# Output projection: the next tile's load and split are written ahead of the present tile's matmuls

## The chip, the cores and the metric

The kernel runs on one core of a Trainium2 chip. A core has a matmul engine (TensorE, PE in the profile; its weight loads are PEld), a vector engine (VectorE, DVE), an activation engine (ScalarE, ACT), GpSimd (POOL) and a queue for issuing DMAs (SyncE, SP). The metric is the device time of one launch in microseconds.

## The reference

One layer of a streaming encoder over 2048 prompt frames, 16 meta tokens and 32 sample frames. Cut to the lines that matter:

```python
q, k, v, z_a, b_g, c_g, u, z_c = split_proj(rmsnorm(hp, norm_g[l]), w_in[l])
...
o = rmsnorm(o, sub_g) * (1.0 - lam_init)
o = o.reshape(*o.shape[:2], W_ATT) * jax.nn.silu(z_a)
y_c = jax.nn.silu(z_c) * b_g * conv_out
return jnp.concatenate([o, y_c], axis=-1) @ w_o
...
y_prompt = rmsnorm(hp[:, N_META:], final_g)
y_sample = rmsnorm(hd, final_g)
```

`o` comes from differential attention with four heads, `conv_out` from a short gated convolution. The concatenation is 1024 wide, `w_o` is 1024x1024; its product is added to the residual `hp`, and the sum goes through a last RMSNorm. The change touches only this last product and what surrounds it.

## The kernel before, in words

Inputs and weights are f32. Each matmul is done in three terms on operands that are split into a high and a low part (hi x hi, lo x hi, hi x lo): the hi part is a cast on ScalarE, the lo part a subtraction on VectorE or GpSimd.

The kernel first runs the input projection and the attention for four blocks of 512 frames and four heads, and leaves the concatenation, transposed, in DRAM (`cat`, one piece for each block; `cat_s` for the sample frames). At the end stands the output projection over tiles of 128 frames: 16 prompt tiles (0 to 13, then 15 and 16 by their place in the list below) and one tile of 32 sample rows (place 14). In this document a tile is named by its place in that list. The columns of the result are done in two halves of 512:

- `out_first` (L700) does the first half of tiles 0 to 11 and puts the sums in DRAM (`y0`), together with the sums of squares of each row. It is spread through the attention work of the last block.
- `out_rest` (L709) does the second half of tiles 0 to 11, then both halves of places 12 to 16, normalises and stores.

For each tile `load_cat` (L660) loads 512 KB of `cat` into a `wraw` buffer, of which there are two, and splits it in two pairs. In `out_rest` the even places put the pairs in `chh` and `cll` (tags `wh`, `wl`, four buffers each) with the lo part on GpSimd. The odd places, called spare, put both in `cs` tiles of the tag `p0`, with the lo part on VectorE. The tag `p0` has twelve buffers (`NP[0]`), and the two result tiles `y` of each tile are `p0` tiles too. A new `p0` tile takes the slot of the oldest, and its writer waits until the last user of that one is done; for a `y` that is its store.

`half_product` (L678) runs 24 matmuls of 128x512 into PSUM, adds the sum to `y` on VectorE (L694) and squares and accumulates it on ScalarE (L695). In `out_rest` L727 adds the sums of squares, `rsqrt` (L178 to L184) goes VectorE, ScalarE twice (L179, L180), VectorE four times (L181 to L184), and L731 scales each half before its store.

All DMAs are issued by SP, in order (L80). The order of the instructions on each engine is fixed when the kernel is built: a scheduler places every instruction from its dependences, and the order in which the code is written is its priority. Each engine then runs its row in order and waits at the head for what is missing.

Of the kernel before, what the change touches and what calls it, by code (L numbers as in the profile page):

```python
# [47 lines left out]
def hybrid_step(ctx: ExitStack, tc: tile.TileContext, x, xT, ckT, cv, scT, rel_bias, norm_g, w_in,  # L48
# [24 lines left out]
    def halved(out, a, b, op, engine=None):  # L73

        n = out.shape[-1] if len(out.shape) == 2 else out.shape[1]
        cuts = (0, n // 2, n) if engine is None and n * (out.shape[-1] if len(out.shape) > 2 else 1) > 256 else (0, n)
        for c0, c1 in zip(cuts, cuts[1:]):
            (engine or G).tensor_tensor(out[:, c0:c1], a[:, c0:c1], b[:, c0:c1], op=op)  # L78
# [97 lines left out]
    def rsqrt(r, ssum, var, w, scale):  # L176

        V.tensor_scalar(var, ssum, scale, EPS, op0=ALU.mult, op1=ALU.add)  # L178
        S.activation(r, var, AF.Ln)  # L179
        S.activation(r, r, AF.Exp, scale=-0.5)  # L180
        V.tensor_tensor(w, r, r, op=ALU.mult)  # L181
        V.tensor_tensor(w, w, var, op=ALU.mult)
        V.tensor_scalar(w, w, -0.5, 1.5, op0=ALU.mult, op1=ALU.add)
        V.tensor_tensor(r, r, w, op=ALU.mult)  # L184
# [459 lines left out]
    def w_half(n):  # L644
        if n == 0:
            his = [xp.tile([P, NX + QT], F32R, tag=f"xh{k}", name=f"woh{k}")[:, :512] for k in range(KT)]
            los = [xp.tile([P, NX + QT], F32R, tag=f"xl{k}", name=f"wol{k}")[:, :512] for k in range(KT)]
        else:
            ks = [ks_tile(c) for c in range(2)]
            his = [ks[k // 4][:, 512 * (k % 4):512 * (k % 4 + 1)] for k in range(KT)]  # L650
            los = [one.tile([P, QT], F32R, tag=f"q{c}{i}", name=f"wq{c}{i}", bufs=2) for _ in range(2) for c in range(2)
                   for i in range(2)]
        for k in range(KT):
            wr = g_tile(512) if n == 1 and k >= 4 else one.tile([P, QT], F32, tag="xt", name="wr", bufs=XB)
            dma(wr, w_out[P * k:P * (k + 1), 512 * n:512 * (n + 1)])
            S.copy(his[k], wr)
            (G if k % 2 else V).tensor_tensor(los[k], wr, f32(his[k]), op=ALU.subtract)
        return his, los

    def load_cat(t, rows, spare=False):  # L660
        ct = wp.tile([P, KT, P], F32, tag="wraw", name="ct")
        dma(ct[:, :, :rows], cat_s if t == 16 else cat[t // 4][:, t % 4])
        parts = []
        for i in range(2):
            c = ct[:, 4 * i:4 * i + 4, :rows]
            if spare:
                chh, cll = [pp.tile([P, 4, P], F32R, tag="p0", name="cs", bufs=NP[0]) for _ in range(2)]
            else:
                chh = wp.tile([P, 4, P], F32R, tag="wh", name="chh", bufs=4)
                cll = wp.tile([P, 4, P], F32R, tag="wl", name="cll", bufs=4) if t < 16 else chh  # L670
            S.copy(chh[:, :, :rows], c)  # L671
            lo = cll[:, :, :rows] if t < 16 else cll[:, :, rows:2 * rows]
            halved(lo, c, f32(chh[:, :, :rows]), ALU.subtract, V if spare or t == 16 else None)
            parts.append((chh, cll))
        hi, lo = ([parts[k // 4][j][:, k % 4] for k in range(KT)] for j in range(2))
        return hi, lo if t < 16 else None

    def half_product(y, c, w, rows, ssq, more=False):  # L678

        chh, cll = c  # L680
        ps = (ps_s if more else ps_j).tile([P, 512], F32, tag="s" if more else "pj", name="po")
        if cll is None:
            for k in range(KT):
                for i in range(2):
                    T.matmul(ps[:2 * rows], lhsT=chh[k][:, :2 * rows], rhs=w[i][k],  # L685
                             start=(k == 0 and i == 0), stop=(k == KT - 1 and i == 1))
            lo = g_tile(512)[:rows]
            S.copy(lo, ps[rows:2 * rows])
            V.tensor_tensor(y, lo, y, op=ALU.add)
        ps = ps[:rows]  # L690
        for k in range(KT if cll is not None else 0):
            for i, (a, b) in enumerate(((chh, w[0]), (cll, w[0]), (chh, w[1]))):
                T.matmul(ps, lhsT=a[k][:, :rows], rhs=b[k], start=(k == 0 and i == 0), stop=(k == KT - 1 and i == 2))  # L693
        V.tensor_tensor(y, ps, y, op=ALU.add)  # L694
        S.activation(g_tile(512)[:rows], y, AF.Square, accum_out=ssq)  # L695

    def rows_of(t):
        return (NS, 0) if t == 16 else (P, NX + P * t)

    def out_first(ts, w):  # L700
        for t in ts:
            rows, x0 = rows_of(t)
            c = load_cat(t, rows)
            y = g_tile(512)[:rows]
            dma(y, x[x0:x0 + rows, :512])
            half_product(y, c, w, rows, ssq0[:rows, t:t + 1])
            dma(y0[t][:rows], y)

    def out_rest(ts, done, w0):  # L709
        w1 = w_half(1)  # L710
        fg = [pp.tile([P, 512], F32, tag="p1", name="fg", bufs=NP[1]) for _ in range(2)]
        for n in range(2):
            dma(fg[n], final_g[512 * n:512 * (n + 1)].partition_broadcast(P))
        for t in ts:
            rows, x0 = rows_of(t)
            c = load_cat(t, rows, ts.index(t) % 2 == 1)
            y = [pp.tile([P, 512], F32, tag="p0", name="y", bufs=NP[0])[:rows] for _ in range(2)]
            if t in done:
                dma(y[0], y0[t][:rows])
            else:  # L720
                dma(y[0], x[x0:x0 + rows, :512])
                half_product(y[0], c, w0, rows, ssq0[:rows, t:t + 1])
            dma(y[1], x[x0:x0 + rows, 512:])
            ss = sm.tile([P, 1], F32, tag="ss", name="ss")[:rows]
            half_product(y[1], c, w1, rows, ss, True)
            var, rs, w = (sm.tile([P, 1], F32, tag=f"y{i}", name=f"y{i}")[:rows] for i in range(3))
            V.tensor_tensor(ss, ss, ssq0[:rows, t:t + 1], op=ALU.add)  # L727
            rsqrt(rs, ss, var, w, 1.0 / D)
            dst = y_s if t == 16 else y_p[P * t:P * (t + 1)]
            for n in range(2):  # L730
                V.scalar_tensor_tensor(y[n], y[n], rs, fg[n][:rows], op0=ALU.mult, op1=ALU.mult)  # L731
                dma(dst[:, 512 * n:512 * (n + 1)], y[n])
# [27 lines left out]
    w0 = w_half(0)  # L760
    first = list(range(12))
    out_first(first, w0)
    out_rest(list(range(12)) + [12, 13, 16, 14, 15], first, w0)

_INS = ["x", "xT", "ckT", "cv", "scT", "rel_bias", "norm_g", "w_in", "conv_w", "lam_in", "subln_g", "w_out",
# [47 lines left out]
```

## Time and profile before

| | |
|---|---|
| time, three runs | 1292.02, 1292.07, 1293.26 us, median 1292.07 |
| profiled execution | 1293.26 us, its span 1291.5 us |
| TensorE busy | 1267.5 us (98%), mean granted clock 0.995 |
| VectorE, ScalarE, GpSimd busy | 923.9 us (72%), 827.5 us (64%), 699.0 us (54%) |
| DMA | 198.74 MB, 154 GB/s |
| chain that ended last | TensorE 55%, VectorE 3%, DMA 3%, ScalarE 1% |

The busy shares are means over the whole span. The span is from the first to the last instruction; the profiled execution's own time is 1.8 us longer. The output projection's second half takes the last 150 us.

### The profile page before, as it was taken

The page shows a single profiled execution, that of the slowest core. Times are in us where ns is not written, and L with a number is a line of the kernel's source. Part 1 is how long each engine was busy: PE and PEld are TensorE (multiplying, and loading weights), DVE is VectorE, ACT ScalarE, POOL GpSimd, SP SyncE. Part 2 cuts the span into 40 slices and gives each one's busy share as a digit, 9 for nine tenths or more (in the row PEclk, how much of TensorE's full clock was granted, in tenths as well). Part 3 has the DMA queues.
Part 4 walks back from the last instruction along what each step waited for, and adds up shares of the span by engine and source line. Part 5 has one row for each costly group of instructions (what it writes and reads, how often), then busy time and mean ns, then how long its engine had stood idle before and what let it go on. Part 6 is the DMA issues. An engine that isn't in the chain of part 4 may idle for free.

```text
span 1291.5 us, 21630 instructions
## 1 busy us (share of the span) xinstructions
PE 1267.5 (98%) x7058; PEld 1101.4 (85%) x7058; DVE 923.9 (72%) x2086; ACT 827.5 (64%) x2030; POOL 699.0 (54%) x918
## 2 busy tenths in 40 slices
PE   8999999999999998999999999999999999999897
PEld 6999999988888886888888888888888888888675
DVE  8767566567886847787878677767786896856654
ACT  6745454675776647677767567777777786763322
POOL 5775857767565675455556555364656483432200
PEclk9999999999999999999999999999999999999999
DMA  9834444774445347444343453344334543557652
GB/s 290 226 116 129 141 112 116 216 241 149 137 117 159 125 145 228 156 137 134 101 169 124 142 177 114 116 147 119 117 109 141 177 133 124 177 181 237 215 181 81
DMA packets 108048, 198.74 MB, mean 154 GB/s; under 512 B 17408, under 2 KB 45600, under 8 KB 107936
## 3 DMA queue, kind: packets, MB, share of 16 engines
q1 hardware_dynamic: 107936, 197.37, 49.0%
q8 instruction: 55, 0.90, 0.3%
q14 instruction: 57, 0.47, 0.1%
HBM read 145.62 MB, written 43.26 MB: 146 GB/s over the span
## 4 chain that ended last, share of the span: by engine, by line
PE 55%; DVE 3%; DMA 3%; ACT 1%; issue 1%; DVEq 0%; SPq 0%; ACTq 0%
PE pj L225 27%; PE po L693 9%; PE s L446 4%; PE s L447 4%; PE pt L462 3%; PE po L469 2%; PE po L471 2%; PE po L470 2%; DMA out<-y 1%; DMA ct<-cat 1%; PE po L685 1%; DMA y<-y 0%; DVE y L731 0%; PE ptv L316 0%; DVE cs L78 0%
## 5 line engine op out<-in xcount | busy, mean ns | idle before, releaser
L78 POOL TENSOR_TENSOR wl<-wr,wh 128x256 fp32r<-128x256 f32 x480 | 377.4, 810 | 300.6 <-ACT wh L204 279.4
L225 PE MATMUL pj<-xh,wh 128*128 128x512 f32 (+2 forms) x1280 | 456.9, 358 | 3.0 <-DVE g L352 1.3
L225 PE MATMUL pj<-xl,wh 128*128 128x512 f32 (+2 forms) x1280 | 453.6, 355 | 0.9 <-DVE xl L153 0.9
L225 PE MATMUL pj<-xh,wl 128*128 128x512 f32 (+2 forms) x1280 | 452.9, 354 | 0.0
L225 PEld LDWEIGHTS pj<-xh,wh 128*128 128x128 f32 x1280 | 242.5, 190 | 34.8 <-issue 2.3
L225 PEld LDWEIGHTS pj<-xh,wl 128*128 128x128 f32 x1280 | 242.2, 189 | 29.9 <-issue 0.2
L225 PEld LDWEIGHTS pj<-xl,wh 128*128 128x128 f32 x1280 | 242.4, 189 | 29.5 <-DVE xl L153 1.4
L397 ACT ACTIVATE p<-s,nm 128x384 f32<-128x384 f32 (+5 forms) x352 | 208.6, 595 | 68.8 <-DVE nm L396 41.9
L204 ACT CAST wh<-wr 128x512 fp32r<-128x512 f32 x256 | 157.5, 618 | 102.7 <-PE pj L225 72.0
L401 DVE SCALAR_TENSOR_TENSOR p<-p,cf,p 128x384 f32<-128x384 f32 (+5 forms) x176 | 127.1, 751 | 23.9 <-ACT p L400 23.7
L396 DVE TENSOR_REDUCE nm<-s 128x1 f32<-128x384 f32 (+3 forms) x224 | 122.6, 560 | 22.7 <-PE s L447 22.5
L78 POOL TENSOR_TENSOR cll<-ct,chh 128x256 fp32r<-128x256 f32 x80 | 63.1, 815 | 131.2 <-ACT chh L671 131.2
L466 DVE TENSOR_TENSOR al<-pt,ah 128x512 fp32r<-128x512 f32 x144 | 97.2, 684 | 46.7 <-ACT ah L465 46.1
L446 PE MATMUL s<-ks,q 128*128 128x384 f32 (+5 forms) x352 | 127.3, 363 | 1.0 <-ACT p L397 0.8
L447 PE MATMUL s<-ks,q 128*128 128x384 f32 (+5 forms) x352 | 122.5, 349 | 0.0
L400 ACT ACTIVATE p<-p,cf 128x384 f32<-128x384 f32 (+5 forms) x176 | 99.1, 623 | 28.2 <-DVE cf L377 25.3
L465 ACT CAST ah<-pt 128x512 fp32r<-128x512 f32 x144 | 81.2, 585 | 42.7 <-PE pt L462 41.6
L393 DVE CUSTOM_DVE_ANT_0 s<-s,bz 128x512 f32<-128x512 f32 (+5 forms) x128 | 74.7, 588 | 21.5 <-PE s L447 19.0
L462 PE MATMUL pt<-ident,p 128*128 128x128 f32 x544 | 86.0, 272 | 0.0
L470 PE MATMUL po<-al,vh 128*128 128x256 f32 x288 | 82.5, 287 | 0.0
L469 PE MATMUL po<-ah,vh 128*128 128x256 f32 x288 | 81.7, 284 | 0.0
L471 PE MATMUL po<-ah,vl 128*128 128x256 f32 x288 | 81.2, 282 | 0.0
(237 smaller groups left out, 2192.2 us busy)
## 6 DMA issues: line engine op xcount, KB each, us to landing
wr<-in_w_in SPq DMA_DIRECT2D x128, 512.0 KB, 3.7
ct<-cat SPq DMA_DIRECT2D x28, 512.0 KB, 4.7
q<-q SPq DMA_DIRECT2D x64, 128.0 KB, 2.9
out<-y SPq DMA_DIRECT2D x32, 256.0 KB, 3.6
ks<-ksd SPq DMA_DIRECT2D x8, 776.0 KB, 5.3
xr<-in_x SPq DMA_DIRECT2D x24, 256.0 KB, 4.9
out<-g SPq DMA_DIRECT2D x24, 256.0 KB, 3.3
xt<-in_xT SPq DMA_DIRECT2D x24, 256.0 KB, 4.9
```

Source lines behind the costliest of these rows:

```text
L78: (engine or G).tensor_tensor(out[:, c0:c1], a[:, c0:c1], b[:, c0:c1], op=op)
L204: S.copy(wh, wi)
L225: T.matmul(ps, lhsT=a[:, k % 4], rhs=b[k][:, b0:b1], start=(k == 0 and i == 0), stop=(k == KT - 1 and i == 2))
L396: V.tensor_reduce(nm[:, c, j:j + 1], s, op=ALU.min, axis=AX.X)
L397: S.activation(pr[j][c], s, AF.Exp, bias=nm[:, c, j:j + 1], scale=-1.0, accum_out=l[:, c, j:j + 1])
L401: V.scalar_tensor_tensor(a0, a1, cf[:, 1, j:j + 1], a0, op0=ALU.mult, op1=ALU.add)
L446: T.matmul(ps, lhsT=qd[c][0][:, qs], rhs=ks[c][:, col:col + w], start=True, stop=False)
L447: T.matmul(ps, lhsT=qd[c][1][:, qs], rhs=ks[c][:, col:col + w], start=False, stop=True)
L462: T.transpose(pt[:, i, P * qi:P * (qi + 1)], cols(aa[qi], NM + P * (2 * j + i), P), ident)
L469: T.matmul(po, lhsT=vh[:, kt], rhs=ah[:, i], start=(kt == 0), stop=False)
L470: T.matmul(po, lhsT=vh[:, kt], rhs=al[:, i], start=False, stop=False)
L693: T.matmul(ps, lhsT=a[k][:, :rows], rhs=b[k], start=(k == 0 and i == 0), stop=(k == KT - 1 and i == 2))
```

## The change

In both loops `load_cat` of the first tile is called ahead of the loop, and inside it the next tile's `load_cat` is called before the present tile's `y` tiles are allocated and its `half_product` is written. Which places are spare stays the same.

```diff
     def out_first(ts, w):
-        for t in ts:
+        nxt = load_cat(ts[0], rows_of(ts[0])[0])
+        for i, t in enumerate(ts):
             rows, x0 = rows_of(t)
-            c = load_cat(t, rows)
+            c = nxt
+            if i + 1 < len(ts):
+                nxt = load_cat(ts[i + 1], rows_of(ts[i + 1])[0])
             y = g_tile(512)[:rows]
...
-        for t in ts:
+        nxt = load_cat(ts[0], rows_of(ts[0])[0])
+        for i, t in enumerate(ts):
             rows, x0 = rows_of(t)
-            c = load_cat(t, rows, ts.index(t) % 2 == 1)
+            c = nxt
+            if i + 1 < len(ts):
+                nxt = load_cat(ts[i + 1], rows_of(ts[i + 1])[0], i % 2 == 0)
             y = [pp.tile([P, 512], F32, tag="p0", name="y", bufs=NP[0])[:rows] for _ in range(2)]
```

The number of instructions of each engine stays the same. ScalarE's row before, from L695 of tile 5: `ct_15153` is tile 10, `ct_15095` is tile 9, `y_14930` is tile 6's second half.

```order
L695 ACTIVATE g_14900,ss_14873<-y_14870 128x512
L671 CAST chh_15155<-ct_15153 128x512
L179 ACTIVATE y1_14903<-y0_14902 128x1
L180 ACTIVATE y1_14903<-y1_14903 128x1
L671 CAST chh_15160<-ct_15153 128x512
L695 ACTIVATE g_14960,ss_14933<-y_14930 128x512
L671 CAST cs_15097<-ct_15095 128x512
L179 ACTIVATE y1_14963<-y0_14962 128x1
L671 CAST cs_15101<-ct_15095 128x512
L180 ACTIVATE y1_14963<-y1_14963 128x1
```

The same place after: `ct_15105` is tile 10, `ct_15047` is tile 9, `y_14940` is tile 6's second half.

```order
L695 ACTIVATE g_14912,ss_14885<-y_14882 128x512
L671 CAST chh_15107<-ct_15105 128x512
L179 ACTIVATE y1_14915<-y0_14914 128x1
L180 ACTIVATE y1_14915<-y1_14915 128x1
L671 CAST cs_15049<-ct_15047 128x512
L671 CAST chh_15112<-ct_15105 128x512
L671 CAST cs_15053<-ct_15047 128x512
L695 ACTIVATE g_14970,ss_14943<-y_14940 128x512
L179 ACTIVATE y1_14973<-y0_14972 128x1
L180 ACTIVATE y1_14973<-y1_14973 128x1
```

The two `cs` casts of tile 9 now stand on either side of the second cast of tile 10, and both ahead of L695 of tile 6.

SP's row before, from the stores of tile 1 on: `ct_14977` and `ct_15035` are tiles 7 and 8, `y_14693` and `y_14694` are tile 2, `y_14869` and `y_14870` tile 5.

```order
L80 DMA out_0<-y_14633 128x512
L80 DMA out_0<-y_14634 128x512
L80 DMA ct_14977<-cat1_137 128x1024
L80 DMA out_0<-y_14693 128x512
L80 DMA y_14869<-y0_5_149 128x512
L80 DMA out_0<-y_14694 128x512
L80 DMA y_14870<-in_x 128x512
L80 DMA ct_15035<-cat2_138 128x1024
L80 DMA y_14929<-y0_6_150 128x512
L80 DMA y_14930<-in_x 128x512
L80 DMA out_0<-y_14751 128x512
```

The same place after: `ct_14929` and `ct_14987` are tiles 7 and 8, `y_14703` and `y_14704` are tile 2, and `y_14821` and `y_14822` are tile 4, `y_14881` and `y_14882` tile 5.

```order
L80 DMA out_0<-y_14645 128x512
L80 DMA out_0<-y_14646 128x512
L80 DMA ct_14929<-cat1_137 128x1024
L80 DMA y_14821<-y0_4_148 128x512
L80 DMA y_14822<-in_x 128x512
L80 DMA ct_14987<-cat2_138 128x1024
L80 DMA out_0<-y_14703 128x512
L80 DMA y_14881<-y0_5_149 128x512
L80 DMA out_0<-y_14704 128x512
L80 DMA y_14882<-in_x 128x512
L80 DMA out_0<-y_14763 128x512
```

Tile 8's load has moved ahead of tile 2's stores and of tile 5's `y` loads, and tile 4's `y` loads have moved behind tile 1's stores. In the changed file, L727 and L731 stand at L733 and L737.

## Rows read from the trace of the kernel before

**Rows 1.** Waits of TensorE: total us, times, longest us.
```profile
PE po L693 <- ACT cs L671: 3.2, 2, 2.0
PE po L693 <- DVE cs L78: 0.5, 2, 0.2
```

**Rows 2.** TensorE timeline: start, us, instruction, idle time before it.
```profile
1208.75 0.40 PE L693 MATMUL po<-wq,chh 128*128 128x512 f32 x1
1211.19 0.50 PE L693 MATMUL po<-ks,cs 128*128 128x512 f32 x1 [2.04 <-ACT cs L671]
1211.91 0.50 PE L693 MATMUL po<-ks,cs 128*128 128x512 f32 x1 [0.22 <-DVE cs L78]
...
1224.22 0.40 PE L693 MATMUL po<-wq,chh 128*128 128x512 f32 x1
1225.81 0.50 PE L693 MATMUL po<-ks,cs 128*128 128x512 f32 x1 [1.18 <-ACT cs L671]
1226.53 0.50 PE L693 MATMUL po<-ks,cs 128*128 128x512 f32 x1 [0.23 <-DVE cs L78]
```

**Rows 3.** Windows: length, busy of each engine, clock, DMA share, rate.
```profile
1210.00:1215.00 5.00, 3.59 (x10) 2.61 (x11) 2.90 (x9) 1.50 (x6) 0.00 (x0) 0.75 0.62 204
```

**Rows 4.** Chain that ended last: start, us, what.
```profile
1190.29 4.76 DMA out<-y
...
1197.81 6.17 DMA ct<-cat
...
1209.07 4.06 DMA out<-y
...
1222.85 2.26 DMA out<-y
...
1261.71 22.19 PE po L693 x96
```

**Rows 5.** Timeline of ScalarE, 1204 to 1211.
```profile
1204.07 0.62 ACT L671 CAST chh<-ct 128x512 fp32r<-128x512 f32 x1 [3.94 <-DMA ct<-cat]
...
1204.83 0.20 ACT L180 ACTIVATE y<-y 128x1 f32<-128x1 f32 x1
...
1209.44 0.63 ACT L695 ACTIVATE g<-y 128x512 f32<-128x512 f32 x1 [3.90 <-DVE y L694]
...
1210.52 0.62 ACT L671 CAST cs<-ct 128x512 fp32r<-128x512 f32 x1 [0.35 <-DMA out<-y]
```

**Rows 6.** Timeline of VectorE, 1205 to 1212.
```profile
1205.06 0.46 DVE L181 TENSOR_TENSOR y<-y 128x1 f32<-128x1 f32 x1 [3.38 <-ACT y L180]
...
1206.95 1.86 DVE L731 SCALAR_TENSOR_TENSOR y<-y,y,fg 128x512 f32<-128x512 f32 x2
...
1211.17 0.69 DVE L78 TENSOR_TENSOR cs<-ct,cs 128x512 fp32r<-128x512 f32 x1 [0.62 <-ACT cs L671]
```

**Rows 7.** SP timeline, stores of tiles 4, 5 and 6.
```profile
1200.87 0.57 SPq L80 DMA_DIRECT2D out<-y  x1
...
1208.17 0.33 SPq L80 DMA_DIRECT2D out<-y  x1
...
1215.50 0.84 SPq L80 DMA_DIRECT2D out<-y  x2
```

**Rows 8.** DMA issues: count, size, median us to landing.
```profile
out<-y SPq DMA_DIRECT2D x32, 256.0 KB, 3.6
ct<-cat SPq DMA_DIRECT2D x15, 512.0 KB, 5.0
...
out<-y SPq DMA_DIRECT2D x1, 256.0 KB, 5.8
```

**Rows 9.** Waits of all engines, 1140 to 1291.5.
```profile
ACT chh L671 <- DMA ct<-cat: 15.5, 6, 4.5
...
ACT cs L671 <- DMA out<-y: 8.8, 6, 3.2
```

**Rows 10.** Timeline of TensorE at the matmul of L479.
```profile
1182.27 0.28 PE L479 MATMUL po<-am,ms 96*128 96x256 f32 x1
```

## The prediction

> **What bounds the kernel now.** I read the waits of TensorE over the last 150 us first, because the diff touches the output projection alone. They hold two sources only: 3.2 us for the hi casts `cs` of L671 on ScalarE, 0.5 us for the lo halves `cs` on VectorE [rows 1]. Everywhere else in that stretch TensorE is fed, so a change here is worth at most what hangs on these four waits. TensorE's own rows show where they are [rows 2]: tile 8 ends with the matmul at 1208.75, and tile 9, a spare one (odd, its split lies in `p0` slots), starts at 1211.19; tile 10 ends at 1224.22 and tile 11, spare again, starts at 1225.81. The price is more than the idle time. The windows give a granted clock of 0.75 of full speed, so in part the 1.2 GHz level, in the 5 us around the first stall [rows 3]. The whole price: undisturbed, 96 matmuls take 22.19 us [rows 4], 0.2311 us each; from 1208.98 (the slot after 1208.75) the 50th next matmul, the second of tile 11, would start at 1208.98 + 49 x 0.2311 = 1220.30. It starts at 1226.53. So the two stalls cost 6.23 us: 2.04 + 0.22 + 1.18 + 0.23 = 3.67 idle; 1.68 between 1211.91 and 1224.22 (46 steps, 10.63 us at full pace, 12.31 in the trace); and 0.88 at the edges, where the first matmul of a group, 0.50 long, doesn't overlap with the next. After that TensorE runs full to the end at 1283.9, and what follows (add, square, rsqrt chain, scale, store) starts from its last matmul [rows 4], so it only moves.
>
> Why tile 9 is late, from the chain of waits and ScalarE's rows: the load of tile 10 is issued at 1197.81 and needs 6.17 us [rows 4]. Its first cast waits 3.94 us for it, at the head of ScalarE, and L180 of tile 5 stands behind that cast, at 1204.83 [rows 5]. VectorE waits 3.38 us for L180 and scales tile 5 at 1206.95 [rows 6]. ScalarE then takes L695 of tile 6, after 3.90 us of waiting, and only at 1210.52 the `cs` cast of tile 9, released by a store `out<-y` [rows 5]: the spare slots are shared with the `y` tiles, and this slot is free when the first half of tile 5 has landed. Tile 12's load and tile 7's store, issued at 1222.85 [rows 4], repeat the pattern ahead of tile 11. So load, cast, rsqrt, scale, store and slot make one loop of two tiles, and it is slower than TensorE's 48 x 0.2311 = 11.1 us.
>
> **The change, part by part.** *Work.* Every instruction of before is there after, none is new; casts, splits, loads and matmuls are as many. Nothing is added to any engine's sum. In `out_first` the written order moves, but the engines' rows come out the same; cost 0, as TensorE is the engine that the others wait for there. In TensorE's row eleven matmuls of tile 1's second half move ahead of as many of tile 2's, where it has no wait now; they cost 0 if tile 1's split is ready, and its load is issued no later than before.
>
> *Slots.* With the next tile's `cs` allocated before the present tile's `y`, the first `cs` pair of tile 9 takes the slots that tile 4's stores leave, not tile 5's. At before's own times: tile 4's stores are issued from 1200.87 [rows 7] and need 5.8 us [rows 8], so the first lands near 1206.7. The cast (0.62) ends at 1207.3, VectorE's half (0.69 by [rows 6]) at 1208.0; TensorE wants them at 1208.98. The second pair waits for tile 5's first store, which landed just before the cast at 1210.52 [rows 5]: cast to 1211.1, lo half to 1211.8, wanted 12 matmuls after the first, 1208.98 + 12 x 0.2311 = 1211.75. So even if no load came earlier, stall 1 goes, with nothing to spare.
>
> *Loads.* SP issues the load of tile 8 ahead of the stores of tile 2 and the `y` loads of tile 5, as the rows of SP's order show, and so on down the row. `wraw` has two buffers, and a load still waits for the splits of an earlier tile, so only the head start counts. Following the waits back through the new order with before's durations puts the loads of tiles 4 to 9 some 2 to 6 us sooner, and tile 10's between 1193 and 1196, not 1197.81. Take 1195: landed at 1200 (median 5.0 [rows 8]), cast at 1200.6, L180 of tile 5 at 1200.8. From L180 to the first store it was 1204.83 [rows 5] to the store at 1208.17 [rows 7], 3.3 us: the store goes out at 1204.1, lands at 1207.7 (median 3.6 [rows 8]), and the second pair of tile 9 stands at 1208.3 and 1209.0, wanted at 1211.75: 2.7 us of slack. Tile 6's store then goes out about 1212.6 and lands at 1216.2, the first pair of tile 11 stands at 1217.5, wanted at 1220.07. For the second pair tile 12 must be loaded: issued at 1209.0, when tile 9's split has freed its buffer, landed at 1214.0, L180 of tile 7 at 1214.9, store 1218.2, landed 1221.8, cast at 1222.4 and lo half at 1223.1, wanted at 1222.84 and 1223.07. That is just in time.
>
> *The added wait.* On ScalarE, L695 of tile 6 now stands behind the second `cs` cast of tile 9, and so behind tile 5's store. Behind L695 wait L179 and L180 of tile 6, its scale on VectorE, its store, and the first `cs` of tile 11, which takes the slot of that store. Bounds: at before's times L695 starts at 1211.1, not 1209.44, 1.7 us late. The rsqrt and the scales after it take about 4 us (1205.06 to 1208.81 [rows 6]), so tile 6's store goes out about 1215.3, as before (1215.50 [rows 7]). If it needs the 5.3 us that the chain's slower stores come near to (4.06 to 4.76 [rows 4], 5.8 [rows 8]), the cast of tile 11 ends at 1221.4 and its lo half at 1222.1; TensorE wants them at 1220.07 and 1220.30. That is the worst of this side: 1.8 us of idle, and a second pair perhaps 0.5 later, with up to 1.7 us of half clock and edges again, as at the first stall. The gain is then 6.2 - 1.8 = 4.4 down to 6.2 - 4.0 = 2.2. The other end is the walk with the early load, without a stall: 6.2. I take 5.6, near the upper end: the walk uses median landings, and the 0.6 stands for the second pair of tile 11, which is just in time there.
>
> ScalarE queues strictly in order; the Trainium skill ("TensorE: Matmul & The Clock Gate", Architectural detail, on engine queue depths) says so of ScalarE and VectorE, and it is the rule that speaks against the change: what is put ahead of L695 delays it even when L695's data are there. The trace agrees, L180 at 1204.83 waits out a cast [rows 5]. By that rule alone, the loads no earlier, the sum is the 2.2 to 4.4 above.
>
> Store landings are between 2.26 us [rows 4] and 5.8 us [rows 8]. The 5.8 us ones were issued at 1200.87 [rows 7], inside the 6.17 us of tile 10's load. An earlier load that meets an earlier store could cost that store up to 3.5 us, and with no relief anywhere the gain falls to 5.6 - 3.5 = 2.1. The Trainium skill ("DMA: Bandwidth & Descriptors", Issuing engines are not separate DMA queues) says that all transfers run on the same 16 engines and interleave. No run here yet shows one alone against one beside a load.
>
> **The sum.** 1293.26 (profiled execution; its span is 1291.5) - 5.6 = 1287.7. That execution is 1.2 us above the median 1292.07, and from the median it is 1286.5.
>
> **Rivals.**
>
> A, the forecast: both stalls go, or at most 1 us stays: 1285.9 to 1287.2.
>
> B: stall 1 goes, tile 11 still comes late, because store landing and the L695 behind the cast keep the loop's pace. Gain 2.1 to 4.4: 1287.7 to 1290.0, its middle 1288.8. For it: ScalarE's 8.8 us of waits on `out<-y` are six waits, not two [rows 9], and the slot sharing is not removed. Against: the slot is one half tile older.
>
> C: no change, 1292. The `cs` of tile 9 would be ready no sooner, since the load isn't what released it (the store was, at 1210.52), and the load only waits longer in its buffer; the 15.5 us of `chh` waits on loads [rows 9] are then ScalarE's alone. Against: those waits hold L180 of tile 5 and so the store itself.
>
> D, the other side: ScalarE's new order makes TensorE wait. The place is L478, the cast before the meta matmul L479: L479 at 1182.27 is a single matmul with no idle time before it [rows 10]. In the changed order L478 stands behind the second `cs` cast of tile 5 and L695 of tile 2, that is, behind tile 1's first store. By the walk it starts near 1181.2, about 0.6 us before it is too late. If that store lands 3.5 us late, TensorE stands some 2.9 us and pays half clock like at the first stall (1.68 + 0.4): 5 us, and if the tail's stalls remain too (B at its worst, 2.1 gained) the time is 1292.07 + 5 - 2.1 = 1295. It decides from a landing of about 0.6 us beyond the walk; it ends slower only if tile 11 is late as well.
>
> **Numbers.** A 0.58, B 0.24, C 0.11, D 0.07. What a measurement of this kernel can tell from no change is 0.2%, 2.6 us, so 1289.5 to 1294.7 counts as same. Faster: A and some four fifths of B, 0.78; same: C, the rest of B and a little of D, 0.16; slower: most of D, 0.06. The range goes from 1285.0 (0.9 below a full gain, for starts that differ elsewhere) to 1290.5, which takes in A and B; C and D stay outside.
>
> **What would show it.** Right: no idle before tile 9 and tile 11 in TensorE's waits, granted clock 1.00 through 1210 to 1215, the first `cs` cast of tile 9 done before 1208.9 and the second before 1211.7, loads of tiles 5 to 10 issued earlier. B: one wait left before tile 11, on `cs`, its cast released by `out<-y`, with L695 behind a `cs` cast. C: the two stalls at their old places. D: a new TensorE wait on `am` near 1182. I am wrong if TensorE is idle at a place that has no wait now, or if its last matmul ends before 1277.0, since 1283.9 - 6.2 = 1277.7 is all that I see to gain.

## The result and the profile after

The changed kernel takes 1286.63 us (median of 5 runs, 1284.89 to 1287.25) against 1292.42 us (1292.02 to 1293.89). The ratio is 0.9947, 95% interval 0.9935 to 0.9959: faster by 0.53%, more than the 0.2% that the prediction took as what a measurement can tell from no change. The forecast was 1286.5 us. The profiled execution has a span of 1285.3 us.

TensorE's waits from 1140 us to the end are an empty list after; the four of [rows 1] are gone. Its timeline (start, us, instruction) at the places of [rows 2] has no idle time in brackets:

```profile
1208.91 0.39 PE L693 MATMUL po<-wq,chh 128*128 128x512 f32 x1
1209.14 0.62 PE L693 MATMUL po<-ks,cs 128*128 128x512 f32 x2
...
1219.99 0.39 PE L693 MATMUL po<-wq,chh 128*128 128x512 f32 x1
1220.22 0.62 PE L693 MATMUL po<-ks,cs 128*128 128x512 f32 x2
```

Tile 9 follows tile 8, and tile 11 follows tile 10, each after 0.23 us. The window of [rows 3] has TensorE busy throughout, at full clock:

```profile
1210.00:1215.00 5.00, 5.00 (x23) 4.04 (x23) 1.62 (x4) 1.20 (x3) 1.44 (x2) 1.00 0.83 285
```

The chain that ended last, which in [rows 4] went through loads and stores, is now TensorE alone from 1189.18 to its last matmul:

```profile
1189.18 58.92 PE po L693 x255
1248.10 7.41 PE po L685 x32
1255.51 22.19 PE po L693 x96
```

255 matmuls in 58.92 us are 0.2311 us each, the full pace. The last matmul ends at 1277.70, not 1283.90: 6.20 us sooner. What follows it is as long as before, 1291.5 - 1283.9 = 7.6 us and 1285.3 - 1277.7 = 7.6 us.

ScalarE's row at the place of [rows 5]:

```profile
1198.88 0.62 ACT L671 CAST chh<-ct 128x512 fp32r<-128x512 f32 x1 [0.25 <-DMA ct<-cat]
...
1199.63 0.20 ACT L180 ACTIVATE y<-y 128x1 f32<-128x1 f32 x1
1202.15 0.62 ACT L671 CAST cs<-ct 128x512 fp32r<-128x512 f32 x1 [2.31 <-DMA out<-y]
...
1204.35 0.62 ACT L671 CAST cs<-ct 128x512 fp32r<-128x512 f32 x1 [1.06 <-DMA out<-y]
1204.88 0.63 ACT L695 ACTIVATE g<-y 128x512 f32<-128x512 f32 x1
...
1212.52 0.62 ACT L671 CAST chh<-ct 128x512 fp32r<-128x512 f32 x1 [2.86 <-DMA ct<-cat]
1213.05 0.20 ACT L180 ACTIVATE y<-y 128x1 f32<-128x1 f32 x1
1214.52 0.62 ACT L671 CAST cs<-ct 128x512 fp32r<-128x512 f32 x1 [1.28 <-DMA out<-y]
...
1218.29 0.60 ACT L671 CAST cs<-ct 128x512 fp32r<-128x512 f32 x1
```

The `cs` casts of tile 9 stand at 1202.15 and 1204.35 (before: 1210.52 and 1211.14), those of tile 11 at 1214.52 and 1218.29. They still wait for stores `out<-y`, and a cast of tile 12 still holds up L180 of tile 7 at 1212.52. The waits have not gone; they end in time.

### The profile page after: what moved, and what is told of

The parts are those of the page before. It is cut to its first block, busy times and chain, and to the rows that moved or that the text cites. A ratio compares the mean times of both kernels' runs of the same rounds, so it can differ in the third digit from the quotient of the medians.

```text
span 1285.3 us, 21646 instructions
## 1 busy us (share of the span) xinstructions
PE 1264.1 (98%) x7058; PEld 1099.2 (86%) x7058; DVE 921.1 (72%) x2086; ACT 827.9 (64%) x2030; POOL 699.6 (54%) x918
## 4 chain that ended last, share of the span: by engine, by line
PE 59%; DVE 1%; ACT 1%; DMA 0%; issue 0%; DVEq 0%; ACTq 0%
PE pj L225 27%; PE po L693 14%; PE s L446 4%; PE s L447 4%; PE pt L462 4%; PE po L469 2%; PE po L471 2%; PE po L470 2%; PE po L685 1%; DMA xr<-in_x 0%; PE ptv L316 0%; PE pm L474 0%; DVE p L401 0%; ACT p L397 0%; PE pss L423 0%; PE pss L424 0%
```

## The experiments

In the changed kernel the first pair of tile 9 waits for tile 4's stores and that of tile 11 for tile 6's; in the kernel before they wait for tile 5's and tile 7's. This is read from the slots and dependences of the built kernels. They show too that a slot doesn't go strictly by age: before, the `y` tiles of tile 8 take tile 4's slots, the first hi half and the last lo half of tile 9 take tile 5's, and its other two halves take slots of tile 7's split. The experiments ask whether these slots are the cause (theory S), or the loads that now go out sooner (theory L), or that work is written ahead of the matmuls at all (W).

Two versions needed no run, since their instruction rows are those of a kernel that has one. With the change in `out_rest` alone every engine's row is that of after; with it in `out_first` alone, that of before. So nothing of the gain is in `out_first`. Line numbers shift with the edits: L671 (the casts) is L673 in late_a, late2_a and late_b, L675 in own_slots_b and own8_b, and L678 in deep_b; the other lines of the output projection shift likewise.

**Split ahead of the matmuls, but behind the `y` loads** (y_loads_first).

```diff
             c = nxt
+            y = [...]
+            dma(y[0], y0[t][:rows] if t in done else x[x0:x0 + rows, :512])
+            dma(y[1], x[x0:x0 + rows, 512:])
             if i + 1 < len(ts):
                 nxt = load_cat(ts[i + 1], rows_of(ts[i + 1])[0], i % 2 == 0)
-            y = [...]
```

> The splits of the next tile are still written ahead of the present tile's matmuls, but the present tile's two y loads are written ahead of them, so that y takes its p0 slots first, as before. Theory S (the gain is which p0 slots the spare tiles' cs get, and when): the two stalls of TensorE ahead of tiles 9 and 11 come back, about 1292.4 us, within 0.1% of before. Rival W (the gain is that loads and splits are written ahead of the matmuls, as the change says): stalls gone, about 1286.6 us.

Measured: 1292.76 us, ratio 0.9997 (0.9988 to 1.0006). W falls. Although loads and splits are written ahead of all matmuls of the present tile, the engines' rows are those of before, and so are the stalls:

```profile
1212.50 0.50 PE L693 MATMUL po<-ks,cs 128*128 128x512 f32 x1 [2.06 <-ACT cs L671]
1213.22 0.50 PE L693 MATMUL po<-ks,cs 128*128 128x512 f32 x1 [0.23 <-DVE cs L78]
...
1227.07 0.50 PE L693 MATMUL po<-ks,cs 128*128 128x512 f32 x1 [2.67 <-ACT cs L671]
1227.79 0.50 PE L693 MATMUL po<-ks,cs 128*128 128x512 f32 x1 [0.23 <-DVE cs L78]
```

What counts is whether the spare split is written ahead of the previous tile's `y` loads, which take slots of the same tag.

**Only the odd, spare places ahead** (odd_ahead). The even places call `load_cat` in place, as before. The edit is shown against the changed kernel; `out_first` is that of before.

```diff
-            c = nxt
-            if i + 1 < len(ts):
+            c = nxt if i % 2 == 1 else load_cat(t, rows, i % 2 == 1)
+            if i + 1 < len(ts) and (i + 1) % 2 == 1:
                 nxt = load_cat(ts[i + 1], rows_of(ts[i + 1])[0], i % 2 == 0)
```

> Only the odd, spare places of the second half are written ahead; the even ones and the first half are written as before. Theory S: the even places hold no p0 slot for their split, so all of the gain is here: about 1286.6 us, no wait of TensorE on cs after 1140. Rival W: half of the loads are not written ahead, the loads of even tiles (tile 10 and tile 12 head ScalarE in the chain of before) stay late, half of the gain or less: 1289 to 1291 us.

Measured: 1286.22 us, ratio 0.9945 (0.9931 to 0.9959), no wait of TensorE behind 1140. The engines' rows are those of the changed kernel, so this measures it a second time. All of the gain is in the spare places. With only the even places ahead the rows are those of before (not run).

**Old order, spare splits outside `p0`** (own_slots_b).

```diff
             if spare:
-                chh, cll = [pp.tile([P, 4, P], F32R, tag="p0", name="cs", bufs=NP[0]) for _ in range(2)]
+                if t < 5:
+                    chh, cll = [pp.tile([P, 4, P], F32R, tag="p0", name="cs", bufs=NP[0]) for _ in range(2)]
+                else:
+                    chh, cll = [ap.tile([P, 2, 256], F32R, tag=a, name="cs").rearrange(...) for a in ("ah", "al")]
```

> The kernel before, written in its old order, but the spare splits from tile 5 on lie in the ah and al buffers of the attention (two each), which nobody uses by then, instead of p0 slots. Theory S: no cs cast waits for a store out<-y any more; cs of tile 9 is ready by 1204 and the stalls go: 1286 to 1287.5 us, and the loads of even tiles come earlier too, since the splits free wraw sooner. Rival L (the late loads that head ScalarE and hold up L180 are the cause, the slots follow): the loads are issued as in before, tile 9 or 11 still comes late: 1289 to 1292 us.

Measured: 1293.64 us, ratio 1.0003 (0.9994 to 1.0012). Neither theory had this. The chain of waits shows why (start, us, what):

```profile
1191.59 7.36 DMA out<-y
1198.97 0.34 SPq L80
...
1199.42 5.71 DMA ct<-cat
...
1205.21 1.14 ACT chh L675 x2
1206.35 0.53 ACT cs L675
...
1206.92 49.05 PE po L697 x204
```

With the slots of `p0` left to `y`, the `y` loads move up in SP's row; tile 9's stand behind tile 3's stores, not behind tile 5's. One of them stands at SP's head until a store of tile 3 has landed at 1198.95, and the load of tile 8 behind it can only go out at 1199.42. The cast of tile 8 then waits at ScalarE's head, with the second `cs` cast of tile 7 behind it, at 1206.35. The wait for a store has moved to SP. TensorE stands still for 4.5 us, once, in the middle of tile 7.

**Old order, loads with buffers of their own** (deep_b): from tile 4 on `cat` goes to the `xt` buffers.

```diff
+        if deep:
+            cts = [one.tile([P, QT], F32, tag="xt", name="ct", bufs=XB).rearrange(...) for _ in range(2)]
+            for i in range(2):
+                dma(cts[i][:, :, :rows], src[:, 4 * i:4 * i + 4])
+        else:
+            ct = wp.tile([P, KT, P], F32, tag="wraw", name="ct")
```

> The kernel before, written in its old order, but from tile 4 on the loads of cat go to the xt buffers in two halves of 256 KB, four tiles in flight instead of two; the spare splits share p0 slots with y as before. Theory S: tile loads land earlier, ScalarE's waits on ct fall from 15.5 us, but cs of tiles 9 and 11 still waits for a store out<-y; at least one stall stays: 1289 to 1293 us. Rival L: with early loads L180 isn't held up, the stores go out sooner and the stalls go: 1286 to 1287.5 us.

Measured: 1286.83 us, ratio 0.9949 (0.9937 to 0.9962), no stall. Theory S had this wrong. ScalarE's waits on tile loads fall from 15.5 us for `chh` in [rows 9] to 2.1, while those on stores stay:

```profile
ACT cs L678 <- DMA out<-y: 7.6, 4, 3.4
...
ACT chh L678 <- DMA ct<-cat: 2.1, 1, 2.1
```

The first `cs` casts of tiles 9 and 11:

```profile
1202.91 0.61 ACT L678 CAST cs<-ct 128x512 fp32r<-128x512 f32 x1
...
1215.62 0.62 ACT L678 CAST cs<-ct 128x512 fp32r<-128x512 f32 x1 [1.16 <-DMA out<-y]
```

Tile 11 is the clean case: its first pair waits for tile 7's store, as before, but this store is issued at 1212.47, not at 1222.85. Tile 9's first pair waits for no store here, since it got slots of tile 7's split; tile 5's store would have been in time too (issued at 1201.01, landed 4.7 us later, and TensorE wants tile 9 at 1208.75). So loads that are early enough do without the new slots. Tile 10's goes out at 1182.72 here, 15 us sooner than in [rows 4]. Are early loads needed?

**The changed kernel with late loads** (late_a and late2_a). VectorE copies a column of a scaled `y` into the load's buffer first, so that the load waits for it.

```diff
+        if late is not None:
+            V.tensor_copy(ct[:, 0, :1], late[:, :1])
         dma(ct[:, :, :rows], cat_s if t == 16 else cat[t // 4][:, t % 4])
...
-                nxt = load_cat(ts[i + 1], rows_of(ts[i + 1])[0], i % 2 == 0)
+                nxt = load_cat(ts[i + 1], rows_of(ts[i + 1])[0], i % 2 == 0,
+                               done_y.get({8: 3, 10: 4, 12: 6}.get(i + 1)))   # late2_a: {8: 3, 10: 5, 12: 7}
```

> The changed kernel, but the loads of tiles 8, 10 and 12 are made to wait: VectorE first copies one column of the scaled first half of tile 3, 4 and 6 into the load's buffer, so that the loads go out near 1186, 1197 and 1209 us as in before, not at 1180.5, 1192.8 and 1206.6. Theory L (what decides is when the even tiles' loads go out, since their casts head ScalarE and hold up L180): the stalls ahead of tiles 9 and 11 come back in part or in whole, 1288.5 to 1292 us. Theory S (the slots that cs gets decide): no stall, 1286.3 to 1287.3 us.

> As late_a, with the loads of tiles 10 and 12 waiting for tiles 5 and 7, near 1202 and 1216 us, later than in before. Theory L: stalls as long as in before or longer, 1291 to 1296 us. Theory S: 1286.3 to 1287.5 us, as tile 10 is wanted only at 1214.5 and tile 12 at 1225.6.

Measured: late_a 1286.33 us, ratio 0.9950 (0.9938 to 0.9963); late2_a 1286.01 us, ratio 0.9946 (0.9931 to 0.9962). No wait of TensorE in either. In late_a the loads went out later than aimed at, tile 10's at 1201.67. SP's row of late2_a has the loads of tiles 10 and 12 here:

```profile
1202.23 0.33 SPq L80 DMA_DIRECT2D ct<-cat  x1
...
1213.27 0.40 SPq L80 DMA_DIRECT2D ct<-cat  x1
```

Tile 10's load is 4.4 us later than in [rows 4]; the gain is full. Early loads are not needed. But the casts of tile 10 moved behind L180 of tile 5 as well, so one more run was needed.

**The kernel before with the same late loads** (late_b): the same two lines, on the old order, with late2_a's table.

> The kernel before in its old order, with TensorE's row unchanged, but the loads of tiles 8, 10 and 12 wait for the scaled first half of tiles 3, 5 and 7 (VectorE copies one column of it into the load's buffer first). So they go out later than in before (tile 10 near 1203, not 1197.8), and their casts stand behind L180 of the tile that they held up. Loop theory: what costs is that the cast of an even tile waits for its load at the head of ScalarE with L180 behind it; with that link gone the spare slots come free in time although the loads are later: 1286 to 1288 us. Rival theories L (late loads) and S (cs gets the younger slots, as in before): stalls ahead of tiles 9 and 11 as in before or longer, 1291 to 1296 us.

Measured: 1292.19 us, ratio 0.9996 (0.9987 to 1.0005). The loop theory, that breaking any one link is enough, falls. Tile 9 came in time but for 0.23 us (its first lo half), tile 11 did not. Here are TensorE's, ScalarE's, SP's and VectorE's rows in front of tile 11:

```profile
1222.47 1.52 PE L695 MATMUL po<-ks,cs 128*128 128x512 f32 x2 [2.99 <-ACT cs L673]
```

```profile
1221.80 0.62 ACT L673 CAST cs<-ct 128x512 fp32r<-128x512 f32 x1 [4.42 <-issue]
```

```profile
1216.62 0.33 SPq L80 DMA_DIRECT2D y<-y  x1
1217.30 0.34 SPq L80 DMA_DIRECT2D y<-in_x  x1
1217.73 0.86 SPq L80 DMA_DIRECT2D out<-y  x2
```

```profile
1214.62 1.42 DVE L734 SCALAR_TENSOR_TENSOR y<-y,y,fg 128x512 f32<-128x512 f32 x2
```

The `cs` cast of tile 11 waits for tile 7's store, issued at 1217.73 behind two `y` loads; it lands 4.0 us later, just ahead of the cast. VectorE scales both halves of tile 7 in 1.42 us from 1214.62, so the first was ready near 1215.4, and the store then stood some 2.3 us behind the `y` loads of tile 10, which take tile 6's slots and wait for its stores. So a good part of this stall is a wait on SP. In late2_a, where the loads wait for the same tiles, the same cast waits for tile 6's store and stands at 1212.47:

```profile
1212.47 0.62 ACT L673 CAST cs<-ct 128x512 fp32r<-128x512 f32 x1 [2.44 <-DMA out<-y]
```

late2_a and late_b are written alike but for the change: 1286.01 against 1292.19 us. The loads of tiles 10 and 12 wait for the same tiles in both; in late_b these are done later, and the loads go out at 1205.22 and 1218.69. With late loads in both, the gain comes with the new slots: tile 11's split waits for a store that is one tile older. How much of the 6 us is that slot, and how much the store held up on SP, this pair does not separate.

**Splits and `y` both outside `p0`** (own8_b): own_slots_b, and `y` from tile 5 on in the eight `xt` buffers.

```diff
-            y = [pp.tile([P, 512], F32, tag="p0", name="y", bufs=NP[0])[:rows] for _ in range(2)]
+            y = [(one.tile([P, QT], F32, tag="xt", name="y", bufs=XB) if 5 <= t else
+                  pp.tile([P, 512], F32, tag="p0", name="y", bufs=NP[0]))[:rows] for _ in range(2)]
```

> The kernel before in its old order, from tile 5 on with the spare splits in ah and al and the y tiles in the eight xt buffers: no cs waits for a store, and the y loads no longer stand ahead of the tile loads on SP with a wait for a store, as the one at 1198.97 did in own_slots_b. Loop theory (slot, split, wraw, load, cast, L180, scale, store make one loop, and breaking it at any one link is enough): stalls gone, 1285.5 to 1287.5 us. Rival (only the loads' own buffers matter): loads go out as in before, 1289 to 1293 us.

Measured: 1286.80 us, ratio 0.9954 (0.9942 to 0.9967). TensorE's one wait behind 1140 is 0.4 us, for VectorE at L423, in the attention. The loads of tiles 9 and 10 go out later than in before, by about 5 and 4 us (1195.97 and 1197.81 there):

```profile
1201.01 0.80 SPq L80 DMA_DIRECT2D ct<-cat  x2
```

So the rival falls: in the old order too late loads cost nothing once no split waits for a store. (The `y` tiles have other slots here as well, so this is not the split's slot alone.) own_slots_b failed by SP's row, not because slots don't matter.

**Both: the change and deep load buffers** (deep_a): `deep` of deep_b on the changed kernel, from tile 4 on.

> The changed kernel with the xt buffers of deep_b as well: loads earlier still. After the change TensorE waits for nothing behind 1140, so theory and rivals all give no further gain: 1286 to 1287.2 us. A gain of over 1 us would show that TensorE's row hides a wait that the trace doesn't name.

Measured: 1285.82 us, ratio 0.9946 (0.9932 to 0.9959), no wait. That is no more than the change alone gives (ratio 0.9947): without a wait the stretch is TensorE's own work.

## Why the prediction was right, by its steps

**Where the time goes.** The two stalls with their clock and edges were put at 6.23 us; the last matmul is 6.20 us sooner. Idle time alone, 3.67 us, would have missed two fifths of it. late_b shows the same: 0.23 us of idle at tile 9 and 2.99 at tile 11, but a granted clock of 0.65 and 0.66 over 10 us, and the time of before:

```profile
1220.00:1225.00 5.00, 2.53 (x5) 1.78 (x6) 2.41 (x7) 1.98 (x6) 0.00 (x0) 0.65 0.60 185
1225.00:1230.00 5.00, 5.00 (x16) 3.95 (x15) 3.53 (x10) 1.62 (x5) 3.26 (x4) 0.66 0.92 286
```

**The forecast.** 5.6 us of the 6.2 were taken, and the medians differ by 5.8. The 0.6 held back for the second pair of tile 11 wasn't needed: it was cast by 1218.9, not at 1222.4. Tile 12's load went out at 1206.55 where the walk had 1209.0, and tile 7's store landed in 2.0 us, not the median 3.6 (rows below). That the forecast of 1286.5 us lies within 0.2 us of the measured median is in part luck: the gain of the profiled executions, 6.2 us, is the full one, without the 0.6.

**Slots.** The step holds: tile 9's first cast stands at 1202.15, when tile 4's store has landed, and the pair late2_a and late_b shows what it is worth with late loads. Its wording was off in one place: it is not where `cs` is allocated. With the `y` tiles allocated ahead of the split and their loads written behind it, the rows are still those of after (not run); with the loads ahead, those of before. What is written first takes the slot first.

**Loads.** They did go out sooner: tile 10 near 1192.8, not 1197.81. The prediction let the first stall go by the slots alone and took the earlier loads to be needed for the second. That second part is not borne out: in late2_a tile 10's load goes out later than before, and tile 11 is in time. Without the slots early loads can do (deep_b), but they are 15 us sooner there; whether the 5 us that the change gives would be enough, no run shows.

**The added wait.** It is there. L695 of tile 6 starts at 1204.88, right behind the `cs` cast at 1204.35 that waited for a store; but that store had gone out 6 us sooner than in [rows 7], at 1202.22, so L695 is earlier than before by 4.6 us. The lower bound of the sum, a gain of 2.2 to 4.4 us with tile 11 late by 1.8 us or more at before's own load times, was not seen: late_a and late2_a, with loads as late, have no stall, though there the casts of tile 10 stand behind L180 too.

**Store landings.** The prediction left open whether a store is slower beside a load. SP's row after, with the loads of tiles 9 and 10, the stores of tiles 4 and 5, the load of tile 12, and the stores of tiles 6 and 7 (the latter from 1215.87):

```profile
1190.96 2.12 SPq L80 DMA_DIRECT2D ct<-cat  x2
...
1196.15 1.49 SPq L80 DMA_DIRECT2D out<-y  x2
...
1202.22 0.99 SPq L80 DMA_DIRECT2D out<-y  x2
...
1206.55 0.32 SPq L80 DMA_DIRECT2D ct<-cat  x1
...
1208.52 8.87 SPq L80 DMA_DIRECT2D out<-y  x4
```

The issues' own rows (count, size, us to landing) for the load of tile 10, and then for the first stores of tiles 4, 5, 6 and 7:

```profile
ct<-cat SPq DMA_DIRECT2D x1, 512.0 KB, 6.0
```

```profile
out<-y SPq DMA_DIRECT2D x1, 256.0 KB, 6.0
```

```profile
out<-y SPq DMA_DIRECT2D x1, 256.0 KB, 2.1
```

```profile
out<-y SPq DMA_DIRECT2D x1, 256.0 KB, 5.9
```

```profile
out<-y SPq DMA_DIRECT2D x1, 256.0 KB, 2.0
```

The two at 5.9 and 6.0 us were issued while a tile load was under way (near 1192.8 and 6.0 us long, and from 1206.55 on), with `y` loads issued behind it; the two at 2.0 and 2.1 us when no load was. That agrees with what the Trainium skill ("DMA: Bandwidth & Descriptors", Issuing engines are not separate DMA queues) says of transfers that interleave on the same engines. Whether the tile load alone would do it, without the `y` loads, these four don't tell. The 3.5 us that the prediction allowed for it was nearly the whole of it, 3.9; it fell on tiles 4 and 6, where there was slack.

**The rivals.** B (tile 11 still late) was not seen, but its reason shows in VectorE's rows, the lo halves of the first pairs of tiles 9 and 11:

```profile
1202.86 0.69 DVE L78 TENSOR_TENSOR cs<-ct,cs 128x512 fp32r<-128x512 f32 x1
...
1217.56 0.67 DVE L78 TENSOR_TENSOR cs<-ct,cs 128x512 fp32r<-128x512 f32 x1
```

They end at 1203.55 and 1218.23, and TensorE takes them one matmul after the first, at 1209.37 and 1220.45: 5.8 us of slack, then 2.2 (for tile 7 it is 7.9: its lo half ends at 1190.34, wanted at 1198.29). The loop is still slower than TensorE; it started earlier and had more room. With more tiles of this kind the stall could return, which wasn't tried. C (no change) didn't come; half of its reason held, that the store and not the load released the `cs` cast, and it was an older store that helped. D was far off. L478 ran at 1178.97, not 1181.2, and TensorE had no wait there:

```profile
1178.97 0.36 ACT L478 CAST am<-pm 16x256 fp32r<-16x256 f32 x1
```

## What to carry to other kernels

When a rotating buffer is shared by tiles that wait for a store and tiles that TensorE waits for, look at who takes a slot first: writing the urgent one ahead of the other gives it an older slot, and moving it ahead of the matmuls gives nothing by itself. Before an engine's stall is put down to a late load, hold the load late on purpose: here loads held back for the same tiles cost 6 us in one order and nothing in the other. Freeing a slot can move its wait to the issuing queue, where a load that waits for a store holds up every load behind it.

## What was not expected of the hardware

The same stall is not always paid with the clock. In y_loads_first the first stall (2.06 + 0.23 us) left the granted clock at 1.00 in the 5 us behind it, while the nearly equal one of [rows 2] fell to 0.75 by [rows 3], although the engines' rows are the same in both kernels. Three of the windows of y_loads_first, around its first stall, behind it, and around the second (2.67 + 0.23 us):

```profile
1210.00:1215.00 5.00, 2.71 (x11) 1.66 (x10) 2.35 (x7) 2.06 (x6) 0.00 (x0) 1.00 0.80 265
1215.00:1220.00 5.00, 5.00 (x23) 4.07 (x22) 2.98 (x9) 0.72 (x2) 0.00 (x0) 1.00 0.65 181
...
1225.00:1230.00 5.00, 2.71 (x7) 1.95 (x8) 3.62 (x11) 2.06 (x6) 0.00 (x0) 0.83 0.74 221
```

What decides between the two is not settled by these runs.
